# Where the five 64-row expert slots of a mixture-of-experts layer stand in the order of sixteen

## The chip, the cores and the metric

One NeuronCore of one Trainium2 chip runs the whole program in a single launch. The metric is device time in microseconds (us) of one execution. The core's engines are TensorE (PE, with its weight loads as PEld), VectorE (DVE), ScalarE (ACT), GpSimd (POOL) and SyncE (SP), which here mostly issues DMAs. Inputs and outputs are float32; weights stay in HBM and are streamed once for each layer.

## The reference, cut to what matters

Two layers of a bidirectional encoder over 512 tokens of width 1024. Each layer runs a mixer (attention, gated linear attention and an mLSTM), then a mixture of experts, then a gated embedding:

```python
x = x + mix @ w_out[i]
x = x + hier_moe(rms_norm(x, norm_ffn_g[i]), ...)     # 16 experts, 2 of them for each token
gate = sigmoid(rms_norm(x, norm_ple_g[i]) @ w_ple_gate[i])
x = x + gate * (p[i] @ w_ple_proj[i])

# hier_moe: top-1 group of 4, then top-2 experts inside it
for e in range(16):
    a = silu(t @ w_gate[e]) * (t @ w_up[e])           # 1024 -> 512
    y = y + comb[:, e:e+1] * (a @ w_down[e])          # 512 -> 1024
```

512 tokens with two experts each make 1024 rows that are spread over 16 experts, 64 on average. An expert has three weight matrices of 1024 x 512 float32 elements, two MB each.

## The kernel before, in words

**Slots.** `moe` first works out on the device how many rows each expert has, and numbers the experts by that. Sixteen slots (places 0 to 15) are then worked off by a loop that is unrolled in the program; which expert's weights a place loads is a register value, apart from places 0 to 2, which are experts 0 to 2 in any case (`NFIX = 3`, so that their weights can be loaded before the routing is known). The other thirteen experts are sorted by their number of rows, the fullest first. A place has a fixed capacity: places 0 to 10 (`NBIG = 11`) take up to 112 rows, places 11 to 15 up to 64. If an expert has more rows than its place holds, a loop at the end (`tc.For_i` under `tc.If(cnt > 0)`) does it again; a branch steps over that loop's code where it isn't needed.

**Big places (class `Expert`, 112 rows).** Each weight tile is split into a high and a low part, hi on ACT (line 241, reached from `split`), lo on DVE (line 294), and each product is three matmuls hi*hi, lo*hi, hi*lo (lines 330 to 332 in `mm3`). The gate and up products of a place are 48 matmuls of 512 columns, its down product 24. Its rows `xe` are scaled by the norm's gain on DVE (`scale`, line 1533), transposed by PE (`x_T`, line 1548), and split.

**Small places (class `Small`, 64 rows).** The weights are used unsplit: 16 float32 matmuls for gate and up (line 1639; gate goes to one half of the PSUM partitions, up to the other), 8 for down (line 1665). ACT and DVE don't touch the weights at all; only PE reads them. A small place therefore costs little on PE, ACT and DVE, and loads just as many bytes as a big one.

**Order.** Place e's turn in the loop is: gate and up of e, the transposes of e+1, and the down product of e-1. `fetch(e + 2)` gathers the rows of a later place (POOL, indirect DMA), `store` of e-2 scatters its result rows to `yd` in HBM (POOL, indirect DMA, line 1616). Weight tiles are loaded by SP in exactly this order, 1 MB each, six for a place, into a ring of 16 buffers (`e8`, `E8 = 16`); a load is issued as soon as the readers of the buffer's tile of 16 loads ago are done, and as soon as the DMA that had the same completion semaphore (one of eight in turn) has landed.

**After place 15.** Its down product isn't covered by another expert's work. Then `p` and `w_ple_proj` are loaded (line 1669; `ple_load`), split (`ple_prep`: tiles `pT`, `ph`, `pl`), the branch over the overflow loop is taken, `ple_rows` makes 48 matmuls of them (tile `PR`), and X and Y are read back from HBM: Y is what the scatters wrote to `yd`, so its first load (line 1849) waits for the last scatter. DVE adds Y into X (line 1876), PE transposes X (line 387), and the dense product with `w_ple_gate` follows.

**gc.** A small tile `gc` (norm gain, 128 x 8) is read by `Small.x_split`. In layer 0 the next layer's `gc` is loaded by a DMA on ACT's queue (line 1256) after the last such read.

Of the kernel before, what the change touches and what calls it, by code (L numbers as in the profile page):

```python
# [16 lines left out]
OP = mybir.AluOpType  # L17
# [9 lines left out]
BIG = 1e30  # L27
CAP, CAPS, NBIG, NFIX = 112, 64, 11, 3
NSLOT = 64
# [34 lines left out]
def tile_encoder(ctx: ExitStack, tc: tile.TileContext, A, out):  # L64
    nc = tc.nc
    v, s, g, pe = nc.vector, nc.scalar, nc.gpsimd, nc.tensor
# [134 lines left out]
    tie = const.tile([128, 16], F32, name="tie")  # L201
# [1122 lines left out]
    def moe(l, X, rsx, lg3):  # L1324
# [114 lines left out]
        ix, iy, ixs, iys = [small(nm, 16, I32, bufs=1) for nm in ("ix", "iy", "ixs", "iys")]  # L1439
# [12 lines left out]
        cn = small("cn", 16, bufs=1)  # L1452
        after(v.tensor_copy(cn, pos[:, 64:80]))
        c2, se = small("c2", 16, bufs=1), small("se", 16, bufs=1)
        v.scalar_tensor_tensor(c2, cn, 16.0, tie, OP.mult, OP.add)
        v.tensor_tensor(aux, bc(c2.unsqueeze(1), [128, 16, 16]), bc(c2.unsqueeze(2), [128, 16, 16]), OP.is_gt)
# [18 lines left out]
        ov = small("ov", 16, bufs=1)  # L1475
        v.tensor_scalar(ov, se, NBIG - 0.5, float(CAP - CAPS), OP.is_lt, OP.mult)
        v.scalar_tensor_tensor(ov, ov, float(CAPS), cn, OP.add, OP.is_lt)
# [224 lines left out]
        EX = []  # L1702

        def fetch(e):
            if e >= 16:
                return
            m, ic = (CAP if e < NBIG else CAPS), (ix if e < NFIX else ixs)[:, e:e + 1]
            if e < NFIX:
                w_ = lambda nm: A[nm][l, e]
            else:  # L1710
                pv = nc.values_load(pi[0:1, e:e + 1], engines=[mybir.EngineType.SP], min_val=0, max_val=15)
                w_ = lambda nm: A[nm][l][bass.DynSlice(pv, 1)].rearrange("o k n -> (o k) n")
            EX.append((Expert if e < NBIG else Small)(e, w_, gather(ic, e, m), iys[:, e:e + 1], rps[:, e:e + 1], m))

# [6 lines left out]
        for e in range(16):  # L1721
# [7 lines left out]
            if e > 1:  # L1729
                EX[e - 2].store()  # L1730
            if e < NBIG - 1:
                scale(EX[e + 1].xe, after=st["lo"] if e else None)
# [8 lines left out]
            for u in range(4):  # L1741
                cur.gate_up(4 + u)
                if u == (1 if e < NBIG else 3):
                    cur.silu()
                if e == 0 and u == EU:

                    EX[1].x_T()
                    EX[1].x_split(0)
                    EX[1].x_split(1)
# [236 lines left out]
```

## Time and profile before

| what | value |
|---|---|
| median of 3 runs | 1402.2 us (1399.31 to 1402.86) |
| the profiled execution, its own time | 1402.94 us |
| its span in the trace | 1401.2 us |
| PE busy | 1328.9 us, 95% of the span |
| PEld, DVE, ACT, POOL busy | 75%, 75%, 60%, 21% |
| chain that ended last | PE 44%, DVE 5%, ACT 2%, DMA 1% of the span, among others |
| moved by DMA | 304.38 MB, 217 GB/s on average |
| granted TensorE clock | 0.979 of full speed on average |

The trace is one execution. A row of a timeline gives the start, the time that the merged instructions took together, the engine, the line, output tile <- input tiles, the shape and the count; in brackets stands the idle time of the engine before it, and who ended it. The two expert stages lie at about 360 to 631 us and 1047 to 1317 us from the span's start.

### The profile page before, as it was taken

Reading aid. Unit: us, or ns where it says so; the run is one execution under the profiler, and the core shown is the slowest. Engines: PE = TensorE matmul, PEld = TensorE weight load, DVE = VectorE, ACT = ScalarE, POOL = GpSimd, SP = SyncE. Lnnn points to the kernel's source line nnn. Section 1 sums busy time; section 2 is a strip of 40 time slices with the busy share of each in tenths; the row PEclk is TensorE's granted clock in tenths of the full one; section 3 lists DMA queues with packets and bytes.
Section 4 is the critical chain, followed back from the end, with each engine's and each line's share of the span. In section 5 each row is a group of like instructions: output and inputs, shape, how many; then the busy total and the mean of one; then the engine's idle time right before and its main releaser. Section 6 shows DMA issues by size and latency. Waiting matters only on the chain.

```text
span 1401.2 us, 23498 instructions
## 1 busy us (share of the span) xinstructions
PE 1328.9 (95%) x8357; PEld 1049.4 (75%) x8357; DVE 1047.2 (75%) x1954; ACT 844.7 (60%) x1613; POOL 298.5 (21%) x360
## 2 busy tenths in 40 slices
PE   8998999999899999998999989999979999999896
PEld 5787878898577777437977878789966777763485
DVE  5769887467899999217768788875779999971284
ACT  5554566554688888216656546755556888861364
POOL 3234000120324442100032230002104244421000
PEclk9999999999899999999999999999999999999998
DMA  6231224546799999999233111336487999999861
GB/s 172 78 91 46 67 59 110 181 153 233 240 369 381 375 368 364 354 367 322 89 100 92 47 45 61 84 90 229 125 313 255 378 381 377 370 354 372 309 226 61
DMA packets 170274, 304.38 MB, mean 217 GB/s; under 512 B 29408, under 2 KB 68356, under 8 KB 170148
## 3 DMA queue, kind: packets, MB, share of 16 engines
q1 hardware_dynamic: 143712, 280.00, 57.6%
q0 software_dynamic: 8064, 18.99, 4.0%
q10 hardware_dynamic: 18372, 3.79, 1.4%
q8 instruction: 69, 1.13, 0.3%
q14 instruction: 57, 0.47, 0.1%
HBM read 283.93 MB, written 21.17 MB: 218 GB/s over the span
## 4 chain that ended last, share of the span: by engine, by line
PE 44%; DVE 5%; ACT 2%; DMA 1%; issue 1%; POOL 0%; DVEq 0%; ACTq 0%; POOLq 0%
PE mm L330 4%; PE mm L331 4%; PE mm L332 4%; PE zb L478 3%; PE zb L479 3%; PE zb L480 3%; PE zb L330 2%; PE zb L331 2%; PE zb L332 2%; PE mm L1639 2%; PE mm L1072 2%; DMA we<-in_w_expert_down_dram 1%; PE mm L1056 1%; PE zb L1665 1%; PE tp L387 1%
## 5 line engine op out<-in xcount | busy, mean ns | idle before, releaser
L294 DVE TENSOR_TENSOR lo<-we,hi 128x1024 fp32r<-128x1024 f32 x260 | 304.5, 1216 | 6.5 <-ACT hi L241 2.8
L241 ACT ACTIVATE hi<-we 128x1024 fp32r<-128x1024 f32 x260 | 270.9, 1059 | 51.9 <-PE mm L332 27.6
L478 PE MATMUL zb<-hi,Th 128*128 128x256 f32 x576 | 168.5, 293 | 0.0
L479 PE MATMUL zb<-lo,Th 128*128 128x256 f32 x576 | 164.1, 285 | 1.1 <-DVE lo L294 1.1
L480 PE MATMUL zb<-hi,Tl 128*128 128x256 f32 x576 | 162.9, 283 | 0.0
L1616 POOL DMA_INDIRECT yd<-YE,iys x32 | 96.8, 3026 | 181.4 <-ACT YE L241 172.7
L330 PE MATMUL mm<-hi,xhl 128*112 128x512 f32 x320 | 127.0, 398 | 0.6 <-issue 0.6
L331 PE MATMUL mm<-lo,xhl 128*112 128x512 f32 x320 | 126.0, 394 | 0.0
L332 PE MATMUL mm<-hi,xhl 128*112 128x512 f32 x320 | 125.7, 393 | 0.0
L478 PEld LDWEIGHTS zb<-hi,Th 128*128 128x128 f32 x576 | 109.5, 190 | 6.8 <-issue 5.7
L479 PEld LDWEIGHTS zb<-lo,Th 128*128 128x128 f32 x576 | 110.0, 191 | 4.8 <-issue 2.1
L480 PEld LDWEIGHTS zb<-hi,Tl 128*128 128x128 f32 x576 | 109.5, 190 | 2.0 <-issue 1.7
L294 DVE TENSOR_TENSOR lo<-w,hi 128x1024 fp32r<-128x1024 f32 (+3 forms) x62 | 70.6, 1141 | 21.9 <-PE zb L479 18.0
L241 ACT ACTIVATE hi<-w 128x1024 fp32r<-128x1024 f32 (+3 forms) x62 | 58.3, 947 | 36.2 <-PE zb L480 31.4
L1639 PE MATMUL mm<-we,xhl 128*64 128x512 f32 x320 | 74.6, 597 | 2.1 <-DMA we<-in_w_expert_up_dram 2.1
L330 PE MATMUL zb<-hi,ah 128*112 128x512 f32 x176 | 70.4, 402 | 0.0
L331 PEld LDWEIGHTS mm<-lo,xhl 128*112 128x112 f32 x320 | 55.8, 174 | 18.3 <-DVE lo L294 2.1
L332 PE MATMUL zb<-hi,al 128*112 128x512 f32 x176 | 68.8, 391 | 0.0
L331 PE MATMUL zb<-lo,ah 128*112 128x512 f32 x176 | 68.7, 390 | 0.0
L332 PEld LDWEIGHTS mm<-hi,xhl 128*112 128x112 f32 x320 | 55.8, 174 | 17.2
L330 PEld LDWEIGHTS mm<-hi,xhl 128*112 128x112 f32 x320 | 56.0, 175 | 16.7 <-issue 1.0
L241 ACT ACTIVATE P<-mm,nm 128x512 f32<-128x512 f32 x64 | 44.1, 689 | 39.5 <-DVE nm L1041 39.2
(457 smaller groups left out, 3381.4 us busy)
## 6 DMA issues: line engine op xcount, KB each, us to landing
we<-in_w_expert_up_dram SPq DMA_DIRECT2D x64, 1024.0 KB
we<-in_w_expert_down_dram SPq DMA_DIRECT2D x64, 1024.0 KB
we<-in_w_expert_gate_dram SPq DMA_DIRECT2D x62, 1024.0 KB
w<-in_w_in_dram SPq DMA_DIRECT2D x44, 512.0 KB
we<-in_w_ple_gate_dram SPq DMA_DIRECT2D x8, 1024.0 KB
Y<-yd SPq DMA_DIRECT2D x16, 512.0 KB
X<-xd SPq DMA_DIRECT2D x12, 512.0 KB
w<-in_w_out_dram SPq DMA_DIRECT2D x10, 512.0 KB
```

The lines of the kernel that those rows point to most:

```text
L241: i = s.activation(out_, in_, func, **kw)
L294: i = (g if eng == "g" else v).tensor_tensor(l3, src, h3.bitcast(F32), OP.subtract)
L330: i = pe.matmul(ps, ah, bh, start=start, stop=False)
L331: pe.matmul(ps, ah, bl, start=False, stop=False)
L332: return i, pe.matmul(ps, al, bh, start=False, stop=stop)
L387: st["warm"] = pe.transpose(ps[:, k * 128:(k + 1) * 128], rows[:, (4 * q + k) * 128:(4 * q + k + 1) * 128], ident)
L478: pe.matmul(pt[tb], ah[c][:, sl], hi, start=(k == 0 and (by_tb or tb % 2 == 0)), stop=False, skip_group_check=True)
L479: pe.matmul(pt[tb], ah[c][:, sl], lo, start=False, stop=False, skip_group_check=True)
L480: pe.matmul(pt[tb], al[c][:, sl], hi, start=False, stop=(k == nk - 1), skip_group_check=True)
L1072: pe.matmul(ao[64 * i:64 * i + 64, 0:128], av[:, kb, kvh * 64:kvh * 64 + 64], AT[j - 1 + i][:, kb * 128:(kb + 1) * 128], start=(kb == 0), ...
L1616: st["sc"] = g.indirect_dma_start(out=yv[self.n], out_offset=bass.IndirectOffsetOnAxis(ap=self.iyc, axis=0), in_=ye, in_offset=None, bound ...
L1639: pe.matmul(self.pg[64 * c:64 * c + 64], self.x[:, k, :], self.rw[c][:, k % 4, :], start=(k == 0), stop=(k == KD - 1))
```

## The change

Places 3 to 7 become the small ones, and places 8 to 15 are big. So that the emptiest experts fall on them, the sort key changes its sign: the thirteen free experts now come with the emptiest first. The test for an overflow, which compares each expert's rows with its place's capacity, is written for a band of places in the middle (two more instructions on DVE). All that asked for `e < NBIG` asks for `e in SMALL`.

```diff
-CAP, CAPS, NBIG, NFIX = 112, 64, 11, 3
+CAP, CAPS, NSM, NFIX = 112, 64, 5, 3
+SMALL = range(NFIX, NFIX + NSM)
...
-        v.scalar_tensor_tensor(c2, cn, 16.0, tie, OP.mult, OP.add)
+        v.scalar_tensor_tensor(c2, cn, -16.0, tie, OP.mult, OP.add)
...
-        v.tensor_scalar(ov, se, NBIG - 0.5, float(CAP - CAPS), OP.is_lt, OP.mult)
+        v.tensor_scalar(ov, se, -(NFIX + (NSM - 1) / 2), None, OP.add)
+        v.tensor_tensor(ov, ov, ov, OP.mult)
+        v.tensor_scalar(ov, ov, NSM * NSM / 4, float(CAP - CAPS), OP.is_gt, OP.mult)
...
-            m, ic = (CAP if e < NBIG else CAPS), (ix if e < NFIX else ixs)[:, e:e + 1]
+            m, ic = (CAPS if e in SMALL else CAP), (ix if e < NFIX else ixs)[:, e:e + 1]
...
-            EX.append((Expert if e < NBIG else Small)(e, w_, gather(ic, e, m), ...))
+            EX.append((Small if e in SMALL else Expert)(e, w_, gather(ic, e, m), ...))
...
-            if e < NBIG - 1:
+            if e < 15 and e + 1 not in SMALL:
                 scale(EX[e + 1].xe, after=st["lo"] if e else None)
...
-                if u == (1 if e < NBIG else 3):
+                if u == (3 if e in SMALL else 1):
                     cur.silu()
```

PE at the end of layer 0's experts, before: `L1639` is gate and up of place 15, `L1665` down of places 14 and 15, `L1651` the transposes between them.

```order
L1639 MATMUL mm<-we,xhl 64x512 x16
L1665 MATMUL zb<-we,aT 64x512 x4
L1651 MATMUL tp<-ident,a 128x64 x4
L1665 MATMUL zb<-we,aT 64x512 x12
L1680 MATMUL tp<-ident,p 128x128 x8
L1800 TENSOR_LOAD cmi
```

Both down products there are small ones, of 8 matmuls each, behind a small gate and up.

PE at the same place in the changed kernel, the end of the down product of place 15 (lines stand 1 to 3 further down in its file).

```order
L331 MATMUL zb<-hi,ah 112x512 x2
L332 MATMUL zb<-lo,ah 112x512
L333 MATMUL zb<-hi,al 112x512
L332 MATMUL zb<-lo,ah 112x512
L333 MATMUL zb<-hi,al 112x512
L331 MATMUL zb<-hi,ah 112x512
L332 MATMUL zb<-lo,ah 112x512
L333 MATMUL zb<-hi,al 112x512
L331 MATMUL zb<-hi,ah 112x512
L332 MATMUL zb<-lo,ah 112x512
L333 MATMUL zb<-hi,al 112x512
L1683 MATMUL tp<-ident,p 128x128 x8
```

These are the 12 matmuls of the last weight tile, in place of 4 unsplit ones; hi and lo have to be made by ACT and DVE first.

ACT at the end of layer 0's experts, before: `a` is a place's silu, `YE` the copy of its result for the scatter; the next layer's `gc` and the first steps behind the experts follow, up to the branch (`cmi`).

```order
L241 ACTIVATE a<-mm,rps 64x512
L1256 DMA gc<-in_norm_ffn_g_dram 128x8x1
L241 ACTIVATE YE<-zb 64x512 x2
L241 ACTIVATE a<-mm,rps 64x512
L241 ACTIVATE YE<-zb 64x512 x3
L241 ACTIVATE pT<-tp 128x2x256 x2
L1800 TENSOR_LOAD cmi
```

No weight is split there, and `ph` stands only behind the branch.

ACT at the same place in the changed kernel.

```order
L242 ACTIVATE hi<-we 128x1024 x2
L242 ACTIVATE YE<-zb 112x512 x2
L242 ACTIVATE hi<-we 128x1024 x2
L242 ACTIVATE YE<-zb 112x512
L242 ACTIVATE ph<-we 128x1024
L242 ACTIVATE pT<-tp 128x2x256 x2
L242 ACTIVATE ph<-we 128x1024
L1803 TENSOR_LOAD cmi
```

The splits of the last weight tiles now stand there, the two `ph` steps have moved from behind the branch to ahead of it, and the DMA of `gc` stands some eight places earlier in the program, after place 7's rows are split.

## Rows read from the trace of the kernel before

**Rows 1.** Stretches of layer 0: length, busy time of five engines, clock, DMA share, GB/s.

```profile
360.00:380.00 20.00, 18.01 (x134) 10.88 (x135) 18.76 (x61) 11.01 (x15) 10.01 (x17) 0.78 0.56 180
400.00:460.00 60.00, 60.00 (x284) 46.12 (x283) 59.09 (x60) 51.80 (x62) 22.30 (x10) 1.00 1.04 377
460.00:600.00 140.00, 140.00 (x679) 94.38 (x679) 106.54 (x108) 93.88 (x113) 43.88 (x25) 1.00 1.02 367
600.00:620.00 20.00, 18.46 (x92) 7.24 (x90) 2.23 (x4) 3.06 (x5) 1.81 (x2) 1.00 1.04 385
620.00:640.00 20.00, 13.49 (x57) 6.26 (x54) 5.46 (x7) 8.07 (x12) 1.79 (x2) 0.88 0.79 285
```

**Rows 2.** Timeline of PE: transposes of the next place's rows, layer 0, places 11 to 14.

```profile
538.31 0.93 PE L1548 MATMUL tp<-ident,XE 112*128 112x112 f32 x8
556.06 0.71 PE L1625 MATMUL tp<-ident,XE 64*128 64x64 f32 x8
...
570.10 0.71 PE L1625 MATMUL tp<-ident,XE 64*128 64x64 f32 x8
...
576.43 2.80 PE L1639 MATMUL mm<-we,xhl 128*64 128x512 f32 x12
...
583.99 0.71 PE L1625 MATMUL tp<-ident,XE 64*128 64x64 f32 x8
...
595.63 0.71 PE L1625 MATMUL tp<-ident,XE 64*128 64x64 f32 x8
```

**Rows 3.** The page: DMA queue q0 (gathers and scatters) and one weight's loads.

```profile
q0 software_dynamic: 8064, 18.99, 4.0%
...
we<-in_w_expert_up_dram SPq DMA_DIRECT2D x64, 1024.0 KB
```

**Rows 4.** Timeline of PE at the end of layer 0's experts.

```profile
617.92 3.65 PE L1639 MATMUL mm<-we,xhl 128*64 128x512 f32 x14 [1.54 <-DMA we<-in_w_expert_up_dram]
...
626.32 1.94 PE L1665 MATMUL zb<-we,aT 128*64 128x512 f32 x8 [0.69 <-ACT YE L241]
628.81 1.94 PE L1665 MATMUL zb<-we,aT 128*64 128x512 f32 x8 [0.56 <-SPq L1801]
...
637.02 2.04 PE L330 MATMUL mm<-ph,pT 128*128 128x512 f32 x4 [5.25 <-PEq L1801]
```

**Rows 5.** Timeline of PE at the end of layer 1's experts.

```profile
1315.28 1.94 PE L1665 MATMUL zb<-we,aT 128*64 128x512 f32 x8 [0.53 <-DMA we<-in_w_expert_down_dram]
...
1321.17 2.03 PE L330 MATMUL mm<-ph,pT 128*128 128x512 f32 x4 [2.93 <-ACT ph L241]
...
1334.66 1.27 PE L387 MATMUL tp<-ident,X 128*128 128x128 f32 x8 [0.71 <-PE mm L332]
```

**Rows 6.** Groups by line: the two halves of a split (busy, mean ns, idle before).

```profile
L294 DVE TENSOR_TENSOR lo<-we,hi 128x1024 fp32r<-128x1024 f32 x260 | 304.5, 1216 | 6.5 <-ACT hi L241 2.8
L241 ACT ACTIVATE hi<-we 128x1024 fp32r<-128x1024 f32 x260 | 270.9, 1059 | 51.9 <-PE mm L332 27.6
```

**Rows 7.** Timelines of POOL, SP and DVE behind layer 1's experts: last scatter, Y, adds.

```profile
1318.90 0.90 POOL L1616 DMA_INDIRECT yd<-YE,iys  x1 [4.32 <-DVE YE L1613]
...
1326.02 2.12 SPq L1849 DMA_DIRECT2D Y<-yd  x4
...
1333.15 3.52 DVE L1876 SCALAR_TENSOR_TENSOR X<-Y,wrow,X 128x512 f32<-128x512 f32 x5 [1.51 <-DMA Y<-yd]
```

**Rows 8.** Timeline of POOL: scatters of two big places of layer 0.

```profile
528.08 5.40 POOL L1616 DMA_INDIRECT yd<-YE,iys  x1 [4.23 <-ACT YE L241]
...
545.71 0.95 POOL L1616 DMA_INDIRECT yd<-YE,iys  x1 [4.22 <-ACT YE L241]
```

**Rows 9.** Waits of SP's queue: what the load of p waited for (us, times, longest).

```profile
SPq L1669 <- DMA gc<-in_norm_ffn_g_dram: 11.2, 1, 11.2
```

**Rows 10.** Timeline of DVE in layer 0's routing: the overflow test, the first scaling.

```profile
365.69 0.16 DVE L1476 TENSOR_SCALAR ov<-se 128x16 f32<-128x16 f32 x1
...
369.52 1.28 DVE L1533 TENSOR_TENSOR XE<-XE,gain 112x1024 f32<-112x1024 f32 x1 [0.78 <-DMA XE<-xd,ix]
```

More of the change, by code (lines that the diff above doesn't have):

```diff
@@ L1712, in fetch @@
                 w_ = lambda nm: A[nm][l][bass.DynSlice(pv, 1)].rearrange("o k n -> (o k) n")
-            EX.append((Expert if e < NBIG else Small)(e, w_, gather(ic, e, m), iys[:, e:e + 1], rps[:, e:e + 1], m))
+            EX.append((Small if e in SMALL else Expert)(e, w_, gather(ic, e, m), iys[:, e:e + 1], rps[:, e:e + 1], m))
         for e in range(GA):
```

## The prediction, made before the changed kernel had run

> **What bounds the kernel now.** I read the page first: PE is busy for 95% of the span, so at first sight PE is the limit everywhere. The change touches only the two expert stages, so I then read those by stretches [rows 1]. There PE is at 100% from 400 to 600 us, but the DMA share is full too: 1.04 from 400 to 460, 1.02 from 460 to 600, 1.04 from 600 to 620. Two limits lie on top of each other. Which one ends last is seen at the end of the stage: PE's first idle time that a weight load ended is 1.54 us in place 15, and two more short gaps stand between the last matmuls of that place [rows 4]. In layer 1 too the last eight matmuls of the experts begin when the last weight tile has landed [rows 5]. So the ring of 16 buffers gives the loads a lead over PE, that lead is used up just at the end, and the last landing ends the stage.
>
> The two paces explain this. A big place takes PE 556.06 - 538.31 = 17.75 us from one set of transposes to the next; the two periods in which a small gate-and-up meets a big down product take 14.04 and 13.89 us; a purely small one takes 595.63 - 583.99 = 11.64 us [rows 2]. A place loads six tiles of 1.049 MB whatever its size (three matrices, 64 loads each in 32 places), and the gathers and scatters add 18.99 / 192 = 0.099 MB to each tile [rows 3]. At the 367 GB/s of the long stretch [rows 1] a tile takes 1.148 / 0.367 = 3.13 us and a place 18.8 us. So the DMA is behind PE by about 1 us in a big place and by 7 us in a small one.
>
> **What the order of places changes on the way.** Nothing that lasts. The DMA is full from 400 us on in the present order [rows 1]; the only empty stretch is 360 to 380 (share 0.56), when all buffers are full, and it lies ahead of place 3, so small places at 3 to 7 can't use it. The bytes, the gathers and the scatters are the same in number and size together. The five small places now eat most of the lead early: from the start of place 3 they take PE 14.0 + 13.9 + 3 x 11.6 = 63 us, while their 30 tiles take the DMA 94 us, so 31 us of lead go. The present order spends the same 31 us at the end, after eight big places have cost it 8 x 1.05 = 8 us; as PE does wait in place 15, the lead at place 3 must be about 31 + 8 = 39 us less what is left, a little over 12 tiles, which 16 buffers can hold. So after place 7 about 8 us of lead, two or three tiles, should be left, and the eight big places then use them up, 1 us each. PE's sum doesn't change: the periods with a big down product move, and the last landing stays where it is, at about 628.8 and 1315.3 us [rows 4, 5]. I take 0 us for the whole middle. What bounds it: below, the DMA share of 1.02 against 1.04 over 140 us is at most 140 x 0.02 / 1.04 = 2.7 us a layer that a fuller queue could win back; above, with so little lead one late tile, 3.1 us a layer, may reach the end.
>
> **The tail of the last place.** This is what the change costs. After the last tile has landed, a small place needs eight passes on PE, 1.94 us [rows 5]. A big one must split first: hi 1.06 us, then two lo of 1.22 us one after the other (the second hi runs beside the first lo) [rows 6], 3.5 us, and then five matmuls remain. One costs (576.43 - 570.81) / 24 = 0.234 us, 570.81 being the end of the transposes ahead of a big down product of 24 matmuls [rows 2]; five and the last one's drain of some 0.2 us make 1.4. So 4.9 us in place of 1.94: **+2.9 us in each layer**, on the path that ends the stage.
>
> How much of it reaches the end of the kernel is read from what follows.
> - Layer 1: the Y chain. Result copy, scatter at 1318.90, Y's first load at 1326.02, the adds at 1333.15 that waited 1.51 us for Y, then the transposes of X at 1334.66, before which PE had been idle for 0.71 us [rows 5, 7]. Each link is waiting for the one before, so all 2.9 us pass. The scatter may cost more now: two scatters of equal size took 5.40 and 0.95 us on POOL [rows 8]. The splits on DVE ran beside the long one, and in the new order a split of w_ple_proj (`pl`, 1.2 us) stands right behind the last result copy. I take 0.6 us, between 0 and 5.40 - 0.95 = 4.5, near the low end because the last scatters before, which stand at the same place, took 0.90 [rows 7]. Layer 1: +3.5 us.
> - Layer 0: PE was idle for 5.25 us behind the transposes of p, ended by the branch, and then did ple_rows; X was transposed right behind [rows 4]. Layer 1 had 2.93 us there, ended by the split `ph` [rows 5]. The new order does `ph` ahead of the branch. If the wait is the branch's own, all 2.9 us pass; if it was the late `ph`, the wait falls to about 2.9 us and 0.6 us are left. I take +2.0 us.
> - On the branch there is a rule. The trace has a PE idle time of 5.25 us that ends at the branch [rows 4]. The Trainium skill ("Runtime: NRT & Kernel Launch", section "Instruction fetch mechanics") says that a taken branch to code outside the fetched window stalls for a fetch. By it the wait can't be shortened by moving `ph`, and layer 0 would give +2.9 and the kernel 0.9 us more; layer 1, where `ph` ended a shorter wait, speaks for the lesser figure.
> - gc: its DMA, issued late, held the load of p for 11.2 us in layer 0 [rows 9]; it now goes out after place 7. p isn't on the path as long as place 15 is at work, and w_ple_proj lands behind the last weight tile in any case. I credit 0.5 us, between 0 and the longest gap that a load made there, 1.54 [rows 4]. What hides the rest is the last down product; without that cover it would be most of the 11.2 us.
> - The overflow test has two more DVE instructions of 0.16 us [rows 10]. They stand ahead of the first scaling, before which DVE was idle for 0.78 us waiting for a gather [rows 10]: free. Without that cover 0.3 us a layer.
>
> Sum: 2.0 - 0.5 + 3.5 = +5.0 us on the profiled execution's 1402.94, 1407.9 us; that execution lies 0.7 us above the median of the runs, so against 1402.2 it is **1407.2 us**. A measurement of this kernel tells about 0.3%, 4.2 us, from no change: same is 1398.0 to 1406.4.
>
> **The rivals.**
> - *The queue fills.* With a lead of two or three tiles instead of twelve the buffers are free early, SP is no longer held by them, and the DMA share goes from 1.02 to 1.04: 2 x 2.7 us back, 1407.2 - 5.4 = 1401.8, no change. For it: the dip exists. Against it: the share is highest, 1.04, in the stretch where the buffers still hold SP back (400 to 460), and lower when the queue is deep.
> - *Long streams run faster.* If the rate rises clearly in the deep queue, PE alone sets the end: the gaps of 1.54 + 0.69 + 0.56 = 2.8 us in place 15 [rows 4] go in both layers, the last tile no longer comes last, so the tail costs little: 1402.2 - 5.6 = 1396.6 us, faster. It decides once a tile takes under 17.75 / 6 = 2.96 us, 388 GB/s. The stretches give 367 to 385 [rows 1], so it is unlikely. The Trainium skill ("DMA: Bandwidth & Descriptors", section "Bandwidth") gives 341 GB/s for a transfer of 1 MB alone and 425 for 16 MB, which speaks for it; no stretch here reaches that, and the shallow stretch wasn't slower than the deep one.
> - *The lead is too small.* ACT and DVE serve splits, result copies and row splits in one order; with two tiles of lead, a copy queued behind a split whose tile hasn't landed holds PE as well. Price: one tile, 3.1 us, in each layer, 1407.2 + 6.2 = 1413.4 us. For it: eight big places in a row without slack. Against it: PE needs 17.75 us where the DMA needs 18.8, so it can catch up by 1 us a place.
> - *The last scatter is a long one* (5.40 us instead of 0.95 [rows 8]) in both layers: +3.9 in layer 1, up to 4.5 in layer 0, about 1415 us.
> - *The five emptiest don't fit* and the overflow loop runs. The same five experts fill the small places in both orders, so what didn't overflow doesn't now, unless a tie is broken differently; tens of us if it did.
>
> **How the numbers follow.** Forecast 0.50 (1404 to 1411, about a third of it under 1406.4), queue fills 0.22, faster stream 0.08, lead too small 0.10, long scatter 0.08, overflow 0.02. Slower than 1406.4: 0.33 of the forecast and the 0.20 of the last three, 0.53. Within 0.3%: 0.17 of the forecast, 0.20 of the filling queue, 0.03 of the faster stream, 0.40. Faster: 0.05 of the faster stream and 0.02 of the filling queue, 0.07. The range 1400 to 1414 leaves out the faster stream, the overflow and the far part of the long scatter.
>
> **What would show it.** Right: in the profile after, no long PE gap in places 3 to 10, PE idle ended by weight loads from about place 12 on; the last tile's landing within 2 us of 628.8 and 1315.3; about 5 us from the last landing to the end of place 15; Y's first load about 3 us later in layer 1. Wrong: DMA share under 1.0 between 420 and 600 us (then the middle isn't neutral), PE gaps of several us at places 6 to 8 (then the lead was smaller than 12 tiles) with a lower granted clock behind them, or a last landing that moved by more than 3 us.

## The result, and the profile of the changed kernel

The changed kernel takes 1414.8 us (median of four runs, 1411.9 to 1415.6) where the kernel before took 1402.0 in the same measurement: **1.0091 times as long, 95% interval 1.0071 to 1.0111**. That is 12.8 us more, where 5.0 had been forecast; it lies just above the upper end of the range. A second measurement of the changed kernel, among the experiments, gave 1414.9 us and 1.0086 [1.0069, 1.0103].

The profiled execution shows where the time is. I take as the length of an expert stage the time from the first gate-and-up matmul of place 0 to the end of the last down matmul of place 15. Before, the two stages took 258.55 and 257.66 us; now they take 263.95 and 264.73. These 5.40 + 7.07 = 12.47 us are all of the difference of the spans, 1413.5 - 1401.2 = 12.3. Outside the stages the shifts cancel: 1.0 us more between the two, 1.0 us less behind the second.

The stretches of layer 0 that answer to [rows 1] (length, busy time of PE, weight loads, DVE, ACT and POOL with their instructions, granted clock, DMA share, GB/s), and one more behind them:

```profile
360.00:380.00 20.00, 17.37 (x135) 10.75 (x136) 19.48 (x64) 11.24 (x16) 11.09 (x17) 0.83 0.57 184
400.00:460.00 60.00, 60.00 (x296) 31.68 (x296) 27.78 (x30) 24.82 (x32) 12.04 (x13) 1.00 1.03 367
460.00:600.00 140.00, 137.57 (x647) 91.39 (x644) 112.82 (x114) 96.14 (x119) 32.16 (x23) 1.00 1.03 374
600.00:620.00 20.00, 19.48 (x88) 14.19 (x86) 17.17 (x18) 16.07 (x21) 0.94 (x1) 1.00 1.04 393
620.00:640.00 20.00, 16.17 (x75) 11.76 (x73) 16.05 (x17) 14.17 (x18) 3.01 (x2) 1.00 0.65 234
640.00:660.00 20.00, 17.07 (x75) 14.34 (x76) 12.04 (x25) 10.84 (x22) 0.35 (x2) 0.85 0.87 303
```

The DMA is as full as before up to 620 us (1.03, 1.03, 1.04 against 1.04, 1.02, 1.04). From 620 to 640 its share is 0.65, against 0.79 before [rows 1], while PE, DVE and ACT have more to do there than before: the weights are there, and the work on them isn't done. The last expert weights of layer 0 landed at 625.9 us by the trace, 2.9 us earlier than before (628.8), and the stage ended 10.1 us behind that landing, where it had been 2.0. So the end of the stage is no longer the landing of the last weights.

What happens from place 8 on is read best on ACT. Its timeline in layer 0 (start, duration, what is done, and in brackets the idle time ahead of it with what ended it): `hi` is the first half of a weight's split, `a` the silu of a place.

```profile
478.87 1.06 ACT L242 ACTIVATE hi<-we 128x1024 fp32r<-128x1024 f32 x1 [7.56 <-DMA we<-in_w_expert_gate_dram]
...
489.19 1.06 ACT L242 ACTIVATE hi<-we 128x1024 fp32r<-128x1024 f32 x1 [1.72 <-DMA we<-in_w_expert_up_dram]
...
497.48 2.00 ACT L242 ACTIVATE hi<-we 128x1024 fp32r<-128x1024 f32 x2 [1.06 <-DMA we<-in_w_expert_gate_dram]
...
504.95 2.01 ACT L242 ACTIVATE hi<-we 128x1024 fp32r<-128x1024 f32 x2 [1.86 <-DMA we<-in_w_expert_up_dram]
...
525.64 0.69 ACT L242 ACTIVATE a<-mm,rps 112x512 f32<-112x512 f32 x1 [0.81 <-PE mm L333]
...
544.09 0.69 ACT L242 ACTIVATE a<-mm,rps 112x512 f32<-112x512 f32 x1 [0.99 <-PE mm L333]
...
599.41 0.69 ACT L242 ACTIVATE a<-mm,rps 112x512 f32<-112x512 f32 x1 [1.30 <-PE mm L333]
```

The first split of a weight of place 8 had to wait for its landing, at 478.87, and so had others of places 8 and 9. Behind that a place takes (599.41 - 525.64) / 4 = 18.44 us. The big places before took 17.65, and the last of them, ahead of the small ones, the 17.75 of [rows 2]. PE shows hardly a gap in it: its busy time is nearly the whole of each stretch. The record of a matmul lasts 0.39 us, and in an undisturbed row the next one starts 0.23 us later, so a delay of up to 0.16 us between two of them leaves no gap:

```profile
561.45 0.39 PE L333 MATMUL mm<-hi,xhl 128*112 128x512 f32 x1
561.68 0.39 PE L331 MATMUL mm<-hi,xhl 128*112 128x512 f32 x1
```

The number of instructions gives the delays away, as the experiments show below.

The lead itself can be read from the traces: the time from the landing of a place's first gate weights (the last update of that load's completion semaphore) to PE's first matmul of the place. Before, it is about 45 us at place 3 of layer 0, 32.0 at place 8, and 2.6 at place 15. In the changed kernel it is 12.9 us at place 7, 3.0 at place 8, and from there to place 14 between 2.1 and 2.6 us. Two to three us are about what the first split takes (1.06 us for hi, 1.22 for lo [rows 6]). So at place 8 there was no lead left to use, and from there on the weights were used as they landed.

The end of the stages on PE, as in [rows 4, 5]:

```profile
615.05 0.49 PE L332 MATMUL mm<-lo,xhl 128*112 128x512 f32 x1 [0.50 <-DVE lo L295]
...
630.25 0.49 PE L331 MATMUL zb<-hi,ah 128*112 128x512 f32 x1 [0.72 <-ACT YE L242]
...
635.87 1.03 PE L1683 MATMUL tp<-ident,p 128*128 128x128 f32 x8
...
640.71 0.76 PE L331 MATMUL mm<-ph,pT 128*128 128x512 f32 x1 [3.81 <-DVEq L1804]
```

No gap there is ended by a weight's landing. Before, one of the three in place 15 was [rows 4]. PE now works from 610.3 us, its first matmul on weights of place 15, to the end with 1.2 us of gaps in all. Place 15 begins no later than before (611.9 us), but a big place leaves 25.7 us to do from there and not 18.9; at the pace that PE has with a lead (e14_half_early, below) it would have begun 4 to 7 us earlier. Layer 1 ends in the same way (gaps of 0.50 and 0.72 us).

Over the whole kernel the two halves of a split, to be compared with [rows 6]:

```profile
L295 DVE TENSOR_TENSOR lo<-we,hi 128x1024 fp32r<-128x1024 f32 x260 | 306.1, 1220 | 40.3 <-ACT hi L242 36.8
L242 ACT ACTIVATE hi<-we 128x1024 fp32r<-128x1024 f32 x260 | 262.3, 1057 | 54.1 <-DMA we<-in_w_expert_gate_dram 17.0
```

The first halves used to wait mostly for PE, for 27.6 us behind one of its lines alone [rows 6]; now the largest part, 17.0 of 54.1 us, was ended by landings of gate weights. The second halves stood idle for 6.5 us before, and now for 40.3.

One thing more was changed that neither the diff nor my prediction speaks of. A scheduler puts each engine's instructions into an order, by its own estimate of when data are there. For places 9 to 15 it wrote another order than before. ACT in one big place, before:

```
460 L241 ACTIVATE YE<-zb 112x512 x2
461 L241 ACTIVATE hi<-we 128x1024 x4
462 L241 ACTIVATE ah<-tp 128x4x112
463 L241 ACTIVATE a<-mm,rps 112x512
464 L241 ACTIVATE hi<-we 128x1024 x5
465 L241 ACTIVATE xhl<-tp 128x4x112 x2
466 L241 ACTIVATE hi<-we 128x1024 x3
```

and in the changed kernel:

```
470 L242 ACTIVATE YE<-zb 112x512 x2
471 L242 ACTIVATE ah<-tp 128x4x112
472 L242 ACTIVATE hi<-we 128x1024 x4
473 L242 ACTIVATE a<-mm,rps 112x512
474 L242 ACTIVATE hi<-we 128x1024 x4
475 L242 ACTIVATE xhl<-tp 128x4x112 x2
476 L242 ACTIVATE hi<-we 128x1024 x4
```

`ah` (the split of the last place's activations) and `xhl` (the split of the next place's rows) stand ahead of splits of weights that they used to follow: one split less is made ahead of `xhl`, which waits for PE. PE's list differs too: transposes of the next rows stand between matmuls that they used to follow.

### The profile page after: what moved, and what is told of

Same layout as the page of the kernel before. It is cut to its first block, busy times and chain, and to the rows that moved or that the text cites. A ratio compares the mean times of both kernels' runs of the same rounds, so it can differ in the third digit from the quotient of the medians.

```text
span 1413.5 us, 23451 instructions
## 1 busy us (share of the span) xinstructions
PE 1336.2 (95%) x8357; PEld 1046.2 (74%) x8357; DVE 1050.6 (74%) x1958; ACT 838.5 (59%) x1613; POOL 252.9 (18%) x360
## 5 line engine op out<-in xcount | busy, mean ns | idle before, releaser
L295 DVE TENSOR_TENSOR lo<-we,hi 128x1024 fp32r<-128x1024 f32 x260 | 306.1, 1220 | 40.3 <-ACT hi L242 36.8
L242 ACT ACTIVATE hi<-we 128x1024 fp32r<-128x1024 f32 x260 | 262.3, 1057 | 54.1 <-DMA we<-in_w_expert_gate_dram 17.0
L332 PE MATMUL mm<-lo,xhl 128*112 128x512 f32 x320 | 131.3, 410 | 4.7 <-DVE lo L295 3.6
L1619 POOL DMA_INDIRECT yd<-YE,iys x32 | 48.0, 1501 | 235.6 <-ACT YE L242 225.6
L295 DVE TENSOR_TENSOR lo<-w,hi 128x1024 fp32r<-128x1024 f32 (+3 forms) x62 | 70.8, 1144 | 22.1 <-PE zb L480 18.2
L479 PE MATMUL zb<-hi,mh 128*128 128x256 f32 x224 | 65.0, 290 | 1.4 <-DVE X L1164 1.4
L333 PEld LDWEIGHTS mm<-hi,xhl 128*112 128x112 f32 x320 | 56.0, 175 | 13.9
```

The source lines that it names most:

```text
L242: i = s.activation(out_, in_, func, **kw)
L295: i = (g if eng == "g" else v).tensor_tensor(l3, src, h3.bitcast(F32), OP.subtract)
L332: pe.matmul(ps, ah, bl, start=False, stop=False)
L333: return i, pe.matmul(ps, al, bh, start=False, stop=stop)
L479: pe.matmul(pt[tb], ah[c][:, sl], hi, start=(k == 0 and (by_tb or tb % 2 == 0)), stop=False, skip_group_check=True)
L1619: st["sc"] = g.indirect_dma_start(out=yv[self.n], out_offset=bass.IndirectOffsetOnAxis(ap=self.iyc, axis=0), in_=ye, in_offset=None, bound ...
```

## The experiments

All times of a table row are from one measurement, beside the kernel before; the stage lengths are those of the profiled executions, layer 0 and layer 1.

| kernel | small slots at | stages, us | time, us | ratio to before |
|---|---|---|---|---|
| before | 11 to 15 | 258.5, 257.7 | 1402.0 | 1 |
| changed | 3 to 7 | 263.9, 264.7 | 1414.8 | 1.0091 [1.0071, 1.0111] |
| e12_again | 3 to 7 | 264.0, 264.6 | 1414.9 | 1.0086 [1.0069, 1.0103] |
| e1_sort | 11 to 15 | 257.8, 258.4 | 1404.8 | 1.0014 [1.0002, 1.0027] |
| e2_last_small | 3, 4, 5, 6, 15 | 261.6, 261.7 | 1407.2 | 1.0029 [1.0011, 1.0047] |
| e3_last_big | 10 to 14 | 267.5, 267.2 | 1420.6 | 1.0132 [1.0116, 1.0149] |
| e4_spread | 3, 6, 9, 12, 15 | 263.5, 264.7 | 1411.0 | 1.0071 [1.0052, 1.0089] |
| e10_two_last | 3, 4, 5, 14, 15 | 257.2, 257.9 | 1403.8 | 1.0016 [1.0006, 1.0026] |
| e11_four_last | 3, 12 to 15 | 258.1, 257.9 | 1404.8 | 1.0015 [1.0002, 1.0027] |
| e5_text_order | 3 to 7 | 264.9, 264.4 | 1410.2 | 1.0058 [1.0042, 1.0073] |
| e13_text_again | 3 to 7 | 265.7, 265.2 | 1409.9 | 1.0049 [1.0029, 1.0069] |
| e8_l1_text | 3, 4, 5, 6, 15 | 262.9, 261.7 | 1411.1 | 1.0064 [1.0046, 1.0081] |
| e7_half_mid | 3 to 7 | 259.1, 258.9 | 1396.4 | 0.9958 [0.9942, 0.9973] |
| e9_half_last | 3 to 7 | 265.3, 263.8 | 1406.9 | 1.0033 [1.0019, 1.0046] |
| e14_half_early | 3 to 7 | 259.1, 257.1 | 1394.9 | 0.9946 [0.9930, 0.9963] |
| e15_full_lists14 | 3 to 7 | 265.5, 264.7 | 1410.0 | 1.0046 [1.0028, 1.0064] |
| e16_half_lists5 | 3 to 7 | 264.4, 262.9 | 1408.5 | 1.0039 [1.0028, 1.0049] |

Some stages hold a stretch of 3.4 us in which TensorE was granted half of its clock (0.5 in the trace, 1.2 instead of 2.4 GHz). It lies at place 0 in one layer each of e3, e5, e11, e13 and e14, which makes that place 1.0 us longer (14.2 instead of 13.2), and behind a wait of PE in a late place in e2, e3 and e15 (both layers), e4 and e8 (one layer). The kernel before and the changed one have none in their stages. Differences of 1 to 2 us between two stages can come from that.

### Which places, and is it the places at all?

The first four kernels, with e10 and e11 later, are the changed one with a table from place to rank, so that the five emptiest experts can stand on any places:

```
-SMALL = range(NFIX, NFIX + NSM)
+SMALL = (3, 4, 5, 6, 15)        # or 11 to 15, 10 to 14, ...
+RANK = ...                      # ranks 3 to 7 to the places in SMALL, 8 to 15 to the others
...
-            m, ic = (CAPS if e in SMALL else CAP), (ix if e < NFIX else ixs)[:, e:e + 1]
+            r = RANK[e]
+            m, ic = (CAPS if e in SMALL else CAP), (ix if e < NFIX else ixs)[:, r:r + 1]
```

**e1_sort.** 

> The changed kernel with its sort (emptiest first) and its overflow test, but the five small slots on the last places 11 to 15 again, by a table from place to rank. Theory A (the places cost the 12.8 us): 1402, within 2 us of the kernel before. Theory B (the sort, the test or the earlier load of the small vector gc cost part of it): above 1405.

Measured: 1404.8 us, with stages as long as before (257.8 and 258.4 us). Theory A holds for the stages. The sort, the test and what else differs from the kernel before cost 0.14% beside it (0.02 to 0.27%), some 2 us with an interval that nearly reaches zero; they don't lie in the stages. In the profiled executions 2.2 us of it lie between the transposes of X behind layer 0's experts and the next expert stage, 411.4 us against 409.2; what makes them I didn't find.

**e2_last_small.** 

> Small slots on places 3, 4, 5, 6 and 15: as changed, but the last place is small. The changed kernel's PE had 11.4 us of gate-and-up, 5.9 and 5.6 us of down products from the start of place 15, and the kernel before about 10 us less with the same start of place 15 (610.3 and 611.9). Theory A1 (what costs is PE work left when the last tiles land; the middle is free): the last place small takes away some 6 of the 6.4 us of each layer, 1402 to 1405. Theory A2 (what costs is the middle, eight big places without a lead, 18.45 instead of 17.65 us each): at most a small part comes back, 1410 to 1413.

Measured: 1407.2 us, stages of 261.6 and 261.7. Neither theory alone: of the 12.5 us that the stages had lost, 7.1 are left. This kernel had 8.5 us of lead at place 8 (layer 0), about what the prediction gives the changed one. Places 8 to 11 ran at 17.6 to 17.8 us with it; at place 13 the lead was down to 3.2 us, and places 13 and 14 took 18.4 and 19.9 us.

**e3_last_big.** 

> Small slots on places 10 to 14, only the last place big: the lead of the loads is kept until place 10 as before. Theory A1 (PE work left at the end): 3.3 us more in gate-and-up and 2.3 us more in the last down product than before in each layer, less the 1 to 3 us for which PE now waits for tiles there: 1407 to 1412. Theory A2 (middle without lead): 1402 to 1405, since the middle has its lead.

Measured: 1420.6 us, worse than the changed kernel and than both theories. The lead goes in the five small places, 24.1 us at place 11 and 2.3 at place 15, and the one big place behind them has none to use. PE at the start of place 15:

```profile
612.28 0.48 PE L332 MATMUL mm<-hi,xhl 128*112 128x512 f32 x1 [2.30 <-ACT hi L243]
613.54 0.49 PE L333 MATMUL mm<-lo,xhl 128*112 128x512 f32 x1 [0.78 <-DVE lo L296]
```

PE waits for the two splits one after the other, and the same happens again in the last down product (2.27 and 0.53 us). It isn't the big place at the end in itself that costs this, but what it meets: e14_half_early, below, has one and loses nothing.

**e4_spread.** 

> Small slots on places 3, 6, 9, 12 and 15: the lead is used up in steps, and the last place is small. Theory A1: 1401 to 1404. Theory A2: the lead (39 us at place 3 by the prediction) falls by 6 us a small place and 1 us a big one and lasts until about place 14: 1402 to 1405 as well; a time above 1406 would speak against both and for a cost of each change between small and big.

Measured: 1411.0 us. A time above 1406 was to speak against both theories and for a cost of each change between small and big, and the trace shows one: with a small place as every third, the periods from one set of transposes to the next are 14.03, 17.91 and 16.10 us over and over, 48.04 for three places where three big ones take 52.95. A small place alone saves 4.9 us of PE, one within a block 17.65 - 11.64 = 6.0.

### Is it the order that the scheduler wrote?

**e5_text_order** ties PE's instructions of places 8 to 15 to the order in which the code names them, which is the order that the kernel before has there (each matmul and transpose is made to follow the last one on PE, without a semaphore); ACT and DVE are left to the scheduler.

```
+            row["on"] = e >= 8          # in the loop over places
+                if row["on"]:
+                    if row["last"] is not None:
+                        order(row["last"], i)
+                    row["last"] = i
```

> The changed kernel with TensorE's instructions of places 8 to 15 tied to the order in which the code names them. In the changed kernel the scheduler that orders the instructions spreads the transposes of the next x between the matmuls from place 9 on and draws those of a ahead of the next gate-and-up; in the kernel before it keeps the order of the code in the same places. Theory P (this other order holds up PE and ACT): 1402 to 1409. Theory D (the weights' rate holds up places 8 to 15, the order is only its echo): 1412 to 1417.

Measured: 1410.2 us, between the two, but with stages of 264.9 and 264.4 us: what is 4.5 us shorter than in the changed kernel lies behind the stages. **e13_text_again** 

> e5_text_order again, beside the two others on one chip: 1409 to 1412 by all theories.

 gave 1409.9 and **e12_again** 

> The changed kernel again (places by the same table as in the experiments), beside the others on one chip. All theories: 1412 to 1416; a time near e5_text_order's 1410.2 would say that its 4.5 us less were the chip's and not the order's.

 1414.9, so the 4.5 us are the kernel's and not the chip's. About half of them is the wait at the branch: 2.68 us in each layer instead of 3.81. Part of the rest is the row of ple matmuls behind it: from its start to the transposes of X it took 11.0 us where the granted clock was at full (layer 0 of e5, layer 1 of e13), 12.3 to 12.6 with one stretch of 3.4 us at half of it behind the wait (the changed kernel in both layers), and 13.6 with 6.8 us of that (layer 0 of e12). For the stages PE's order alone is not the cause.

**e8_l1_text** is the same for the places of e2_last_small. 

> Small slots on places 3, 4, 5, 6 and 15 as in e2_last_small (1407.2), with TensorE tied to the order of the code from place 8 on. Theory P: 1401 to 1404. Theory D: 1405 to 1409.

Measured: 1411.1 us, stages of 262.9 and 261.7, as long as in e2_last_small within 1.3 us. Here the tied order made the kernel 3.9 us slower, most of it behind the stages, where it gained 4.5 above: both theories missed. Why wasn't tested.

### Is it the weights?

**e7_half_mid**, **e9_half_last** and **e14_half_early** are e5_text_order with less to load: of certain down weights one of two rows is loaded, and used twice.

```
             def load_down(self, k):
+                if 8 <= self.n < 15:    # e9: self.n >= 14; e14: 3 <= self.n < 8
+                    raw = load(wv_[:, k:k + 1, :])
+                    self.rd[k] = self.rd[k + 1] = raw
+                    return
                 raw = load(wv_[:, k:k + 2, :])
```

**e7_half_mid.** 

> As e5_text_order, but of the down weights of places 8 to 14 only one of each two rows of 1024 is loaded and used twice (the output then isn't the reference's): the same matmuls and splits, 1.05 MB of 6.9 MB less for each place, at 3.07 us a tile 3.07 us less. Theory D: places 8 to 14 run at PE's own 17.65 us instead of 18.45, and 6 to 8 us a layer come off e5_text_order, 12 to 16 in all. Theory L (without a lead the lists of ACT, DVE and PE hold each other up, whatever the rate): within 3 us of e5_text_order.

Measured: 1396.4 us, 13.9 less than e5_text_order, stages of 259.1 and 258.9; big places at about 17.65 us again, from place 11 on (17.9 at place 10).

**e9_half_last.** 

> As e5_text_order, but the four down tiles of places 14 and 15, the last expert weights, are loaded to a half only (the output then isn't the reference's), so the last of them lands about 5.6 us earlier. By the prediction (the last landing sets the end of the stage, 4.9 us behind it): 4 to 5.6 us a layer less than e5_text_order. Theory S (PE still has 11.4 + 5.9 + 5.6 us to do from the first weights of place 15 on, more than the loads need): within 2 us a layer of e5_text_order.

Measured: 1406.9 us, stages of 265.3 and 263.8 us against 264.9 and 264.4. The last weights are there earlier (DMA share and GB/s of 620 to 640 us, e5_text_order first, then e9_half_last), and it changes nothing:

```profile
620.00:640.00 20.00, 17.07 (x78) 12.43 (x77) 16.73 (x17) 15.20 (x19) 2.40 (x2) 1.00 0.65 236
```

```profile
620.00:640.00 20.00, 17.62 (x79) 12.75 (x78) 16.46 (x18) 14.81 (x18) 2.00 (x2) 0.98 0.38 128
```

The 3.3 us that the whole kernel gains come behind the stages. So with the order of e5_text_order the landing of the last weights does not set the end of the stage.

**e14_half_early.** 

> As e5_text_order, but the down weights of the small places 3 to 7 are loaded to a half (the output then isn't the reference's): about 15 us of lead more at place 8, while places 8 to 15 load all their bytes at the same rate. Theory G (the lead, not the rate alone): PE runs places 8 to 14 at 17.65 us, a stage of 258 to 260 us, 10 to 14 us less than e5_text_order in all. If big places behind small ones are slow for another reason (their lists, the rate itself while they run): less than 4 us from e5_text_order.

Measured: 1394.9 us, 15.4 less than e5_text_order, stages of 259.1 and 257.1: as short as in the kernel before, with the small slots on places 3 to 7, all weights of places 8 to 15 loaded, and a big place at the end. With a lead of 14.9 us at place 8 instead of 3.1 (e5_text_order, layer 0) nothing is left of the loss. So the big last place costs nothing by itself. That e7 and e14 come out 5 to 8 us below the kernel before, with stages no shorter than its, is time behind the stages; 4.3 us of it are PE's wait at the branch, 2.05 and 1.79 us there and 5.25 and 2.93 before.

**e10_two_last** and **e11_four_last** test the same with all the work done.

> Small slots on places 3, 4, 5, 14 and 15. Stage length from the first to the last matmul of the experts so far: small slots last 258 us (kernel before and e1_sort), on 3, 4, 5, 6 and 15 261.7, on 3 to 7 264.3. Theory G (each small place that is early takes its 6 to 7 us off the lead, and big places wait once about 10 us of lead are left): the lead of 39 us less 18 for three small places less 0.8 for each of eight big ones never falls to 10 us before place 14; what stays is some 1.5 us for the change from a small block back to big places, 259 to 261 us, 1404 to 1407 in all. Theory E (each early small place costs its share, a fifth of 6.2 us): 3.7 us a layer, 1409 to 1411.

> Small slots on places 3, 12, 13, 14 and 15. Theory G: only the change back to big places is left, about 1.1 us a layer (in e4_spread three places with one small among them took 48.04 us on PE, 4.94 less than three big ones, where a small place in a row of small ones saves 6.02): 259 us a stage, 1403 to 1405. Theory E: 1.2 us a layer, the same here.

Measured: stages of 257.2 and 257.9, and of 258.1 and 257.9 us; 1403.8 and 1404.8 us in all, as e1_sort. Theory G, and better than it: three small places of five can stand early at no cost, since the lead lasts (17.0 us at place 8 and 8.5 at place 15 in e10_two_last). The 1.1 to 1.5 us for the change back to big places don't show in the stage. In e10_two_last the waits at its end make up for them: PE's gaps in the last two places are 1.26 us a layer, where the kernel before had 2.8 and 1.8.

### Late weights, or the order written for late weights?

e7 and e14 leave one thing mixed. With less to load the scheduler also writes another order for ACT and DVE, the one of the kernel before. So the two were crossed: **e15_full_lists14** loads everything and has ACT and DVE tied to the order of e14_half_early; **e16_half_lists5** loads as e14_half_early and has the order of e5_text_order.

```
+        for k, x in made.items():       # the instructions of ACT and of DVE in places 8 to 15
+            for a, b in zip(LISTS[l][k], LISTS[l][k][1:]):
+                order(x[a], x[b])       # LISTS: e15 those of e14, e16 those of e5
```

**e15_full_lists14.** 

> All weights loaded as in e5_text_order, but the instructions of ACT and DVE in places 8 to 15 are tied to the order that the scheduler wrote for e14_half_early (one split of a down weight ahead of that of the next x, two more small shifts a place). Theory G (weights behind PE set the pace of places 8 to 14): within 3 us of e5_text_order, 1407 to 1413, stage 262 to 265 us. Theory L (the order that the scheduler writes when it counts on late weights sets it): stage 257 to 260 us, 1394 to 1400.

**e16_half_lists5.** 

> The half-loaded down weights of places 3 to 7 as in e14_half_early (the output then isn't the reference's), with ACT and DVE tied to the order of e5_text_order. Theory G: near e14_half_early, 1394 to 1398, stage 257 to 260 us. Theory L: near e5_text_order, 1406 to 1412, stage 262 to 265 us. A time in the middle gives each its share.

| stages, us | order of e5 (for late weights) | order of e14 (as before) |
|---|---|---|
| all weights | 264.9, 264.4 | 265.5, 264.7 |
| places 3 to 7 half loaded | 264.4, 262.9 | 259.1, 257.1 |

Both theories are right, and neither as it stood. **Each cause alone gives nearly the whole loss, and taking away one of them gives back little:** at most 1.5 of some 7 us, in layer 1 of e16. The waits of ACT say the same in each corner. In e15, from 480 to 600 us (what waited for what: us in all, times, longest):

```profile
ACT hi L105 <- DMA we<-in_w_expert_gate_dram: 14.6, 5, 7.4
ACT hi L105 <- PE mm L83: 10.1, 22, 2.4
ACT hi L105 <- PE zb L83: 3.1, 11, 0.3
ACT hi L105 <- DMA we<-in_w_expert_up_dram: 2.7, 2, 1.7
```

Splits wait for landings, 17.3 us in all, most of it at places 8 and 9: there the order is good and the weights are late. Places 8 and 9 take 20.5 and 20.6 us, against 16.1 and 17.8 in e14; PE's wait there, 3.39 us at the longest, is followed by 3.4 us at half the clock. Behind these waits three places run at 17.65 us, until landings hold them up once more. In e16, same stretch:

```profile
ACT xhl L105 <- PE tp L83: 14.7, 6, 4.3
ACT YE L105 <- PE zb L83: 9.0, 7, 3.1
ACT ah L105 <- PE tp L83: 3.1, 6, 0.6
```

No wait for a landing at all: the weights are there, but in each place ACT stands for 2.1 us at `xhl` until PE has transposed the next rows, with weights behind it in its list that could have been split. Two such places on ACT's timeline, 18.61 us apart:

```profile
566.69 0.98 ACT L105 ACTIVATE xhl<-tp 128x448 fp32r<-128x448 f32 x2 [2.07 <-PE tp L83]
567.55 3.90 ACT L105 ACTIVATE hi<-we 128x1024 fp32r<-128x1024 f32 x4
...
585.30 0.98 ACT L105 ACTIVATE xhl<-tp 128x448 fp32r<-128x448 f32 x2 [2.07 <-PE tp L83]
```

In e14 the same stretch has neither of the two (its 0.6 us at `xhl` came once); splits wait for PE, as before:

```profile
ACT hi L261 <- PE mm L78: 10.0, 36, 0.6
ACT YE L261 <- PE zb L78: 5.5, 2, 3.1
ACT hi L261 <- PE zb L78: 4.2, 15, 0.3
ACT a L261 <- PE mm L78: 2.3, 6, 0.9
```

And PE from 540 to 600 us (length, busy time with instructions, clock, DMA share, GB/s), in the changed kernel, in e16 and in e14:

```profile
540.00:600.00 60.00, 59.48 (x276) 1.00 1.02 379
```

```profile
540.00:600.00 60.00, 59.41 (x274) 1.00 1.03 373
```

```profile
540.00:600.00 60.00, 60.00 (x287) 1.00 1.02 372
```

By busy time the three differ by 1%, by instructions done by 4 to 5%, which is 18.4 to 18.6 against 17.65 us a place.

The lead of each kernel in layer 0, read as above, says the same:

| lead in us at place | 8 | 10 | 12 | 14 |
|---|---|---|---|---|
| before | 32.0 | 29.4 | 23.5 | 8.8 |
| changed | 3.0 | 2.3 | 2.5 | 2.6 |
| e2_last_small | 8.5 | 7.6 | 4.6 | 2.9 |
| e10_two_last | 17.0 | 14.3 | 12.4 | 9.3 |
| e14_half_early | 14.9 | 11.6 | 9.9 | 8.0 |
| e15_full_lists14 | 3.2 | 7.6 | 5.1 | 3.8 |
| e16_half_lists5 | 15.8 | 13.6 | 13.9 | 14.0 |

In e16 the weights are 14 us ahead at place 14, and its places still take 18.6 us. In e14 each place uses up about 1 us of lead, as the prediction has it, and runs at 17.65.

For the changed kernel's own lists, which aren't quite those of e5_text_order, the crossing wasn't made. Its lead is gone at place 8 and never comes back, and behind place 9 its splits still wait for landings, 0.2 to 1.2 us at a time, in layer 1 in every place up to 13. So late weights are the cause that its trace shows; that its lists alone would hold it as well is taken from e16 and not shown for it.

## Why the prediction was wrong, step by step

- **Two limits on top of each other** (PE and DMA): right, but there was a third, the order of ACT's and DVE's lists, which the scheduler writes by its own estimate of when weights land. The prediction compares the two programs at the end of the stage, where it looks for a cost, and not in places 9 to 14, where it expects none.
- **"Nothing that lasts", 0 us for the middle**: this is the step that failed, and within it the account that leaves about 8 us of lead, two or three tiles, after place 7. The traces give 3.0 us in layer 0 and 3.2 in layer 1, about what the first split takes, so nothing was left to spend. At place 3 the lead was larger than the 39 us of the account, about 45, but the 30 tiles of the five small places took 103 us from landing to landing and not 94. The account takes 367 GB/s throughout; the stretches below carried less, the first with the DMA not yet full, the second with it full:

```profile
376.00:400.00 24.00, 24.00 (x115) 18.03 (x114) 24.00 (x26) 19.79 (x23) 8.58 (x4) 1.00 0.89 312
420.00:440.00 20.00, 20.00 (x99) 9.42 (x99) 5.53 (x7) 4.99 (x8) 3.83 (x4) 1.00 1.02 339
```

  Where 8.5 us of lead were really there, in e2_last_small, big places used it up at about 1 us each, as foretold, but it didn't last to the end there either. In the changed kernel places 9 to 14 took 18.2 to 19.0 us instead of 17.65. Layer 1 adds up: places 8 to 14 took 7.0 us more than in e14_half_early, place 15 another 0.6, and the change from small places back to big ones 1.2, which e14 has too; 1.8 us of waits in place 15 that the kernel before had are gone. That makes 7.0, and 7.07 were measured.
- **The last landing stays, and ends the stage**: it came 2.9 us earlier in layer 0, and it doesn't end the stage, which ran on for 10.1 us behind it in both layers, not 4.9. e9_half_last made it earlier still and the stage stayed as long as it was. PE's idle times ended by weight loads from place 12 on, one of the prediction's own signs of being right, are not there. The DMA share under 1.0 that was to show a middle that isn't neutral didn't come either: the middle cost time with the DMA full.
- **+2.9 us a layer for the tail of the last place**: wrong in its mechanism, not only in its size. In e14_half_early the last place is big, and the stage as short as before. The matmuls and splits behind the last tile are there as counted, but PE isn't waiting for that tile; it is still at work on the tiles ahead of it, at its own pace, from the first weights of place 15 (610.3 us) to the end.
- **All of layer 1's delay passes through Y**: it passes, but not through Y. The experts of layer 1 end 13.4 us later than before (1330.6 and 1317.2), the transposes of X come 13.2 us later, at 1347.86 instead of 1334.66 [rows 5]. The last scatter takes POOL 1.47 us instead of 0.90 [rows 7], 0.6 more as forecast. But Y's first load comes only 10.56 us later. It still begins when that scatter has landed; what changed is the landing, 4.3 us behind the issue instead of 6.9, in both layers. Why it is faster wasn't tested. X's transposes now stand on PE right behind the row of ple matmuls that begins at the branch, without a gap. POOL and SP in layer 1:

```profile
1332.05 1.47 POOL L1619 DMA_INDIRECT yd<-YE,iys  x1 [5.02 <-ACT pT L242]
```

```profile
1336.58 2.20 SPq L1852 DMA_DIRECT2D Y<-yd  x4
```

  From issue to landing of the last scatter to `yd` in layer 1, before and in the changed kernel:

```profile
DMA to landing us min/median/max: 6.9/6.9/6.9
```

```profile
DMA to landing us min/median/max: 4.3/4.3/4.3
```

- **The wait at the branch**: the sign was right. PE waits 3.81 us there in both layers now, ended by DVE's arrival at the branch; it was 5.25, and 2.93 behind `ph` [rows 4, 5]. PE's own branch instruction, of two in each kernel (shortest, median and longest in ns, then first and last start in us), before and now:

```profile
L1801 PEldq COMPARE_BRANCH  x2: 1442/3540/5637, 631.1 to 1317.4; - x2
```

```profile
L1804 PEldq COMPARE_BRANCH  x2: 344/2070/3797, 634.8 to 1329.2; - x2
```

  So the 5.25 us of layer 0 were the branch's own, not the late `ph`. In the changed kernel PE has passed the branch, in layer 1 after 0.34 us, and waits for DVE, which has the two splits `pl` ahead of its arrival: the second ends at 640.51 us in layer 0, and PE goes on at 640.71. In all traces this branch of PE took 0.34 to 2.28 us where no 16 KB packet of the instruction queue began while it ran, and 2.94 to 6.50 us where one did. The Trainium skill ("Runtime: NRT & Kernel Launch", section "Instruction fetch mechanics") says that a taken branch out of the fetched window stalls; these packets agree with it.
- **gc and the overflow test**: the test is free, as forecast. No run shows the 0.5 us credited for gc by itself. The first matmul of place 0 comes at 372.1 us, and came at 372.2.
- **Rivals.** The queue doesn't fill beyond 1.03, so nothing comes back. The last scatter isn't long, the overflow loop doesn't run. *The lead is too small* came nearest, 1413.4 us, and had 0.10. The ground on which I made it small, that "PE needs 17.75 us where the DMA needs 18.8, so it can catch up", is wrong by its own numbers: a slower DMA means that PE can never build up a lead. I had also named its price as one late tile, when it is a pace that lasts from place 8 or 9 to place 14; that 1413.4 lies near the measured time is luck in the size.

## What to carry to other kernels

In this kernel the places that use weights faster than the DMA brings them belong at the end of the stage, where the lead can be used up; put first, they take the lead from all that follows, and a big place without a lead took 18.4 instead of 17.65 us with the same work in it, in another order. How much lead a place needs is found by moving the places one by one: three small ones of five stood early at no cost, four cost 3.6 us a layer, five 6.2. It can also be read from the trace, as the time from a tile's landing to its first use. And where a scheduler writes the order, compare the programs also at the places that the change should leave alone, and cross the order with the data before calling one of them the cause: here each alone held the stage at 263 to 265 us.

## What was not expected of the hardware

The DMA's share from 400 to 600 us was 1.00 to 1.05 in every kernel with all its weights, whichever places were small, at 360 to 383 GB/s in stretches of 40 us. The rate of the whole queue didn't depend on who was waiting for it. The Trainium skill ("DMA: Bandwidth & Descriptors", section "Bandwidth") gives 341 GB/s for one transfer of 1 MB and 425 for 16 MB; a full queue of transfers of 1 MB lies between them.

PE's busy time hid the loss: 99% of 540 to 600 us in the changed kernel, in which 276 instructions were done, and 100% in e14_half_early with 287.

POOL's 32 scatters took 1501 ns each in the changed kernel and 3026 before (two of them are in [rows 8]), and the whole kernel was slower: the shorter ones bought nothing here.
